# A two-layer transformer trunk on one core: the three inner layer norms and the first 512 columns of the stage behind each, in a written order of three engines

## The chip, the core and the metric

The kernel runs on one core of a Trainium2 chip. The metric is the device time of one execution in microseconds (us). A core has five engines, each with a queue of its own that runs in the order in which the instructions stand in it: TensorE (PE; its loads of stationary operands are listed apart as PEld), VectorE (DVE), ScalarE (ACT), GpSimd (POOL) and SyncE (SP, which here only issues DMAs). They wait for each other by semaphores.

## The reference

256 tokens of width 2048 pass through two layers. In each, a mixer is added to the scaled stream and normed, then a squared-ReLU MLP of hidden width 8192 is added and normed:

```python
for layer in range(DEPTH):                       # DEPTH = 2
    mix = fox_attention(...) if layer < 1 else nsa_attention(...)
    h = layer_norm(ALPHA * h + mix, ln1_g[layer], ln1_b[layer])
    h = layer_norm(ALPHA * h + sq_relu_mlp(h, mlp_w1[layer], mlp_w2[layer]), ln2_g[layer], ln2_b[layer])
    if layer == 0:
        kv = shared_kv(h, kv_w, ...)             # h @ kv_w: six parts of 512 columns, then compression
```

There are four layer norms. Behind the first and the third stands the MLP's first product (`h @ mlp_w1`, then the square of the ReLU), behind the second the product with `kv_w`, and behind the fourth only the output.

## The kernel before

**Arithmetic.** Each float32 operand is split into a high part (`hi`, the value rounded to the type fp32r) and a low part (`lo`, the rest). A product is hi x hi + hi x lo + lo x hi, accumulated in PSUM. Weights are streamed: `wload` loads half a chunk (128x1024, 512 KB) into one of 4 `raw` buffers, and `fill_split` makes `hi` by a cast on ScalarE (L117) and `lo` by a subtraction on VectorE (L118), into one of 5 `whl` buffers. This splitting goes on through the whole run, on the same two queues as everything else.

**Two forms of product.** In the form of `ws_many` the weights stand still and the 256 tokens stream by: for each of 16 parts of the inner dimension one matmul of 512 columns (L158: w hi against hi and lo of the tokens) and one of 256 (L160: w lo against hi). In the form of `xs_mm` 128 tokens stand still and 512 weight columns stream by: three matmuls of 512 columns for each part of the inner dimension and each half `t` of the tokens (L182). `out_proj` uses the second form for the projections that end in the stream `h`; `done` adds the accumulator to `h` and takes `bn_stats`.

**A junction** is the stretch from the last 512 columns (`n` = 3) of such a projection to the next stage's first products. The function `end` runs it. It keeps the last `LATE` = 4 half chunks of weights in a pool of their own, so that the products of the first 128 tokens (`t` = 0) end before those of the second (`t` = 1). After each half come `done`, `scalars` (mean and 1/sqrt(var + eps): small operations on VectorE, with one square root on ScalarE), then `columns`: two operations of VectorE on each 256 columns (L348 with the gain, L363 with the bias, each a row of 2048 numbers broadcast to 128 partitions by `gains`). `transposer` then turns each 512 columns with 4 matmuls against an identity (L376) into a PSUM tile `pt`, and splits them into the chunk `act` that the next stage reads. The next stage starts in the first form, whose every matmul needs both halves of the tokens. While TensorE has nothing to do there, it runs `tables` (in the first junction: two small products needed later, L597 and L600) or `warm` (in the second and third: `WARM` = 14 matmuls whose result nobody reads, L423). The fourth norm (`final`) divides its columns among VectorE, ScalarE and GpSimd.

**What sets the order.** The instructions are written in program order; a scheduler decides where each stands on its engine by priorities and modelled readiness.

Of the kernel before, what the change touches and what calls it, by code (L numbers as in the profile page):

```python
# [19 lines left out]
P = 128  # L20
S = 256
# [11 lines left out]
LATE = 4  # L33
WARM = 14
# [64 lines left out]
def _trunk(nc, tc, i, out, ctx):  # L99
# [78 lines left out]
    def xs_mm(acc, act, kt, t, w, first, last):  # L178
        s = slice(kt % 2 * 512, (kt % 2 + 1) * 512)
        xh, xl = (act[:, kt, k, t * P:(t + 1) * P] for k in range(2))  # L180
        for n, (l, r) in enumerate(((xh, 0), (xh, 1), (xl, 0))):
            mm(acc, l, w[:, r, s], start=first and n == 0, stop=last and n == 2)  # L182
# [8 lines left out]
    def merge(dst, acc, scale=1.0):  # L191

        t = sp.tile([P, S], F32, tag="mt", name="mt")
# [41 lines left out]
    def out_proj(src, acts, first, ln=None, two=False, between=()):  # L235
# [41 lines left out]
        def end(late, meanwhile=None):  # L277

            ln.gains(late)
            accs = [acc_tile(), acc_tile()]  # L280
            ahead = 8 - LATE
# [5 lines left out]
            ws = [wload(src[3, k // 2], k % 2, late, LATE) for k in range(ahead, 8)]  # L287
            for t in range(2):
                for kt in range(2 * ahead, KT):
                    xs_mm(accs[t], acts[kt // 4], kt % 4, t, ws[kt // 2 - ahead], False, kt == KT - 1)  # L290
# [5 lines left out]
                elif not ln.final:  # L296
                    ln.gained(1, 0)
            after = None
            if meanwhile:
                after = meanwhile()  # L300
            elif not ln.final:
                warm(WARM, ws[0][:, 0, :P], ws[0][:, 0, :512])
            with tc.issue_after(last):
                for t, c in ln.rest:
                    ln.columns(t, c)
                if after:
                    after()
        return end

    class Norm:  # L310


        def __init__(self, li, use, final=False):
            self.li, self.use, self.sc, self.had, self.final = li, use, {}, set(), final
            self.early = (2, 3, 0, 1) if final else (0,)
            self.rest = ((1, 3), (1, 0), (1, 1), (1, 2)) if final else (
                (1, 0), (0, 1), (1, 1), (0, 2), (1, 2), (0, 3), (1, 3))

        def scalars(self, t):
            mv = sp.tile([P, 6], F32, tag="mv", name="mv")  # L320
            nc.vector.bn_aggr(mv[:, 0:2], stats[:, t].rearrange("p c s -> p (c s)"))
            mean, var, v, y, a, rstd = (mv[:, k:k + 1] for k in range(6))
            nc.vector.tensor_scalar_add(v, var, EPS)
# [4 lines left out]
            end = nc.vector.tensor_mul(rstd, y, a)  # L328
            if self.final:
                end = nc.vector.scalar_tensor_tensor(a, mean, -1.0, rstd, op0=OP.mult, op1=OP.mult)  # L330
# [3 lines left out]
        def gains(self, pool):  # L334
            self.gb = []
            for name in ("lng", "lnb"):
                x = pool.tile([P, D], F32, name=name, bufs=1)
# [3 lines left out]
        def pieces(self, t, c):  # L341
            n = 512 if self.final else 256
            return [[x[:, a:a + n] for x in (h[:, t], *self.gb)] for a in range(c * 512, (c + 1) * 512, n)]

        def gained(self, t, c):
            self.had.add((t, c))
            for hs, g, _ in self.pieces(t, c):
                nc.vector.scalar_tensor_tensor(hs, hs, self.sc[t][0], g, op0=OP.subtract, op1=OP.mult)  # L348

        def columns(self, t, c):  # L350
            mean, rstd, nmr = self.sc[t]
            if self.final and (c == 3 or (t, c) == (0, 2)):
                hs, g, b = (x[:, c * 512:(c + 1) * 512] for x in (h[:, t], *self.gb))
# [6 lines left out]
            if (t, c) not in self.had:  # L360
                self.gained(t, c)
            for hs, _, b in self.pieces(t, c):
                nc.vector.scalar_tensor_tensor(hs, hs, rstd, b, op0=OP.mult, op1=OP.add)  # L363
            self.use(t, c)
            if self.final and (t, c) == self.rest[-1]:
                self.use(1, 3)
# [563 lines left out]
```

## Time and profile before

| | us |
|---|---|
| median of 3 runs (2247.07 to 2248.7) | 2247.33 |
| the profiled execution, its own time | 2248.41 |
| its span, first to last instruction | 2246.6 |
| busy in it: TensorE / VectorE / ScalarE | 2220.6 / 1408.0 / 1048.2 |

The page gives the busy time of each engine, then the costliest groups of instructions; a timeline lists the instructions of an engine in order, equal neighbours merged, and in square brackets how long the engine had stood idle and which instruction released it. PEclk is the granted clock of TensorE, 1.00 for 2.4 GHz and 0.50 for 1.2 GHz.

### The profile page before, as it was taken

To read this page: it belongs to the slowest core of one execution; us is meant where nothing else is said; L and a number is where in the kernel's file an instruction comes from. 1 tells how busy PE (TensorE), PEld (TensorE's weight loads), DVE (VectorE), ACT (ScalarE), POOL (GpSimd) and SP (SyncE) were. 2 spreads that over 40 slices of the span, in tenths; PEclk is the share of its full clock that TensorE was granted. 3 is DMA by queue.
4 is the path that set the end of the run, shared out by engine and by line. 5 is a ranking of instruction groups with operands and counts; after the bars stand their busy time and mean duration, and the time that the engine had idled before them with its cause. 6 is when DMAs were issued, how large, how long until landed. Compare 5 with 4: busy or idle time off the path is not lost.

```text
span 2246.6 us, 30144 instructions
## 1 busy us (share of the span) xinstructions
PE 2220.6 (99%) x11478; PEld 1893.7 (84%) x11478; DVE 1408.0 (63%) x2209; ACT 1048.2 (47%) x1564; POOL 18.6 (1%) x26
## 2 busy tenths in 40 slices
PE   9999999999999999999999999999999999999997
PEld 6888888888888888888788899888888888888885
DVE  5665556864665565565786688768655645655655
ACT  4444444443444454454355567544434434444542
POOL 0000000000000000000000000000000000000001
PEclk9999999999999999999999999999999999999999
DMA  7665567566666666666556744565666666666663
GB/s 253 196 197 188 178 188 249 198 190 192 192 191 192 193 188 195 190 188 194 179 165 221 246 134 137 168 217 170 192 192 190 191 193 194 189 193 191 189 196 112
DMA packets 116829, 427.54 MB, mean 190 GB/s; under 512 B 13179, under 2 KB 13339, under 8 KB 115406
## 3 DMA queue, kind: packets, MB, share of 16 engines
q1 hardware_dynamic: 114734, 419.00, 59.5%
q0 software_dynamic: 1952, 6.63, 1.0%
q8 instruction: 90, 1.47, 0.3%
q14 instruction: 53, 0.43, 0.1%
HBM read 423.45 MB, written 4.24 MB: 190 GB/s over the span
## 4 chain that ended last, share of the span: by engine, by line
PE 95%; DVE 2%; DMA 2%; ACT 0%; issue 0%; SPq 0%; ACTq 0%; DVEq 0%
PE acc L182 44%; PE acc L158 31%; PE acc L160 16%; DMA raw<-in_fq 1%; PE pt L839 1%; PE lg L775 0%; PE pt L817 0%; PE pt L376 0%; DMA raw<-in_fv 0%; DVE whl L118 0%; DMA bc<-c_dram 0%; DVE h L363 0%; PE acc L692 0%; PE pt L840 0%; PE pt L533 0%; PE lg L771 0%
## 5 line engine op out<-in xcount | busy, mean ns | idle before, releaser
L118 DVE TENSOR_TENSOR whl<-raw,whl 128x1024 fp32r<-128x1024 f32 (+1 forms) x769 | 938.4, 1223 | 613.6 <-ACT whl L117 605.0
L117 ACT CAST whl<-raw 128x1024 fp32r<-128x1024 f32 (+1 forms) x769 | 805.1, 1048 | 740.3 <-PE acc L182 491.6
L182 PE MATMUL acc<-whl,act 128*128 128x512 f32 x4416 | 1011.7, 390 | 2.2 <-DVE whl L118 1.2
L182 PEld LDWEIGHTS acc<-whl,act 128*128 128x128 f32 x4416 | 827.1, 188 | 177.6 <-DVE whl L118 2.8
L158 PE MATMUL acc<-act,whl 128*128 128x512 f32 x3072 | 757.3, 394 | 0.0
L158 PEld LDWEIGHTS acc<-act,whl 128*128 128x128 f32 x3072 | 563.5, 189 | 107.3 <-issue 0.2
L160 PEld LDWEIGHTS acc<-act,whl 128*128 128x128 f32 x3072 | 398.2, 191 | 16.9 <-DVE whl L118 0.3
L160 PE MATMUL acc<-act,whl 128*128 128x256 f32 x3072 | 408.7, 284 | 0.0
L194 ACT ACTIVATE mt<-acc 128x256 f32<-128x256 f32 x192 | 73.4, 382 | 299.7 <-PE acc L158 297.5
L196 DVE TENSOR_TENSOR mu<-acc,mt 128x256 f32<-128x256 f32 x128 | 54.4, 425 | 113.4 <-ACT mt L194 113.4
L394 DVE SCALAR_TENSOR_TENSOR mu<-mu 128x256 f32<-128x256 f32 x128 | 54.4, 425 | 4.3
L118 DVE TENSOR_TENSOR act<-mu,act 128x256 fp32r<-128x256 f32 x128 | 53.7, 420 | 0.0
L117 ACT CAST act<-mu 128x256 fp32r<-128x256 f32 x128 | 52.1, 407 | 3.1 <-DVE mu L394 1.6
L117 ACT CAST act<-pt 128x256 fp32r<-128x256 f32 x80 | 29.4, 372 | 41.9 <-PE pt L376 31.3
L250 DVE TENSOR_TENSOR h<-h,acc 128x512 f32<-128x512 f32 x48 | 30.9, 681 | 14.2 <-PE acc L182 14.2
L118 DVE TENSOR_TENSOR act<-pt,act 128x256 fp32r<-128x256 f32 x80 | 33.1, 419 | 9.9 <-ACT act L117 9.6
L404 ACT ACTIVATE E<-E,sm 128x128 f32<-128x128 f32 (+1 forms) x64 | 28.9, 453 | 7.8 <-DVE sm L407 7.4
L363 DVE SCALAR_TENSOR_TENSOR h<-h,mv,lnb 128x256 f32<-128x256 f32 (+1 forms) x53 | 26.5, 541 | 0.1
L404 ACT ACTIVATE E<-L,sm 128x128 f32<-128x128 f32 (+1 forms) x32 | 14.3, 449 | 24.8 <-DVE sm L407 24.8
L376 PE MATMUL pt<-cst,h 128*128 128x128 f32 x96 | 19.1, 293 | 6.0 <-DVE h L363 6.0
L348 DVE SCALAR_TENSOR_TENSOR h<-h,mv,lng 128x256 f32<-128x256 f32 (+1 forms) x53 | 25.0, 502 | 0.0
L248 DVE SCALAR_TENSOR_TENSOR h<-h,acc 128x512 f32<-128x512 f32 x32 | 20.6, 681 | 4.2 <-PE acc L182 4.2
(173 smaller groups left out, 664.0 us busy)
## 6 DMA issues: line engine op xcount, KB each, us to landing
raw<-in_w SPq DMA_DIRECT2D x512, 512.0 KB, 3.6
raw<-in_fq SPq DMA_DIRECT2D x32, 512.0 KB, 3.7
raw<-in_fk SPq DMA_DIRECT2D x32, 512.0 KB, 3.6
raw<-in_fo SPq DMA_DIRECT2D x32, 512.0 KB, 4.0
raw<-in_kvT SPq DMA_DIRECT2D x32, 512.0 KB, 4.4
raw<-in_nq SPq DMA_DIRECT2D x32, 512.0 KB, 3.7
raw<-in_no SPq DMA_DIRECT2D x32, 512.0 KB, 4.1
raw<-in_fv SPq DMA_DIRECT2D x31, 512.0 KB, 3.7
```

The costliest lines, as they stand in the source:

```text
L117: nc.scalar.copy(hi, src)
L118: nc.vector.tensor_sub(lo, src, hi.bitcast(F32))
L158: mm(acc, w[:, 0, s], a, start=kt == 0, stop=kt == KT - 1)
L160: mm(acc[:, :S], w[:, 1, s], a[:, 0, :], start=False, stop=False)
L182: mm(acc, l, w[:, r, s], start=first and n == 0, stop=last and n == 2)
L194: nc.scalar.activation(t, acc[:, S:], AF.Copy, scale=scale)
L196: nc.vector.tensor_add(dst, acc[:, :S], t)
L250: nc.vector.tensor_add(hcols(t, n), hcols(t, n), acc)
L348: nc.vector.scalar_tensor_tensor(hs, hs, self.sc[t][0], g, op0=OP.subtract, op1=OP.mult)
L363: nc.vector.scalar_tensor_tensor(hs, hs, rstd, b, op0=OP.mult, op1=OP.add)
L394: nc.vector.scalar_tensor_tensor(u, u, 0.0, u, op0=OP.max, op1=OP.mult)
L404: nc.scalar.activation(E, L, AF.Exp, bias=m, scale=-1.0, accum_out=sums)
```

## The change

The fourth norm keeps its code; only `LATE`, the number of weight half chunks held back, becomes 7 for it too, and its gain and bias tiles come from another pool. The three inner norms get a new function `joined` and a class `Turned`:

- The next stage's first 512 columns (of `mlp_w1`, laid out a second time as `w1r`, or of the part of `kv_w` called `kvN`) are computed in the second form, by halves of the tokens: 96 matmuls into `nxt[0]` and `nxt[1]`, in the order (0,0) (0,1) (0,2) (1,0) (0,3) (1,1) (1,2) (1,3) of pairs (half `t`, 512 columns `c` of the inner dimension), 12 matmuls each. The held weights are 7 half chunks (5 in the first junction, with the `tables` behind the products).
- Each pair has six steps: `norm` on ScalarE (one operation on 128x512, without gain and bias), `turn` on TensorE (4 transposes), `gained` on VectorE and on ScalarE (gain and bias as one number per partition, from `lnT`, on the 128x128 transposes in PSUM; 2 of 4 on VectorE for `t` = 0, 3 of 4 for `t` = 1), `hi` on ScalarE, `lo` on VectorE. `PIECES` gives each step a place. The unit of a place is one matmul of TensorE, and 0 is the first of the next stage.
- Everything in the junction is sorted by place and handed to TensorE, VectorE and ScalarE in that order, past the scheduler; the splits of three of the new weight half chunks stand among it.
- `h` stays without gain and bias for a while; `residual` applies them behind the second 128-column product of the next stage: 8 operations of VectorE on 128x1024, which wait for `lng` and `lnb`.
- In the MLP the two accumulators are 128 tokens by 512 hidden columns. They pass ReLU (ScalarE), square (VectorE), 8 transposes (TensorE) and a split.
- The warm matmuls go. The product with `kvN[0]`, which stood behind the others of its stage, now comes first in it. The buffers of `mt` and `mu` go from 2 to 1.

```diff
-LATE = 4
-WARM = 14
+LATE = 7
+BETWEEN = 11
+PIECES = {
+    (0, 0): (-24, -20, -18, -18, -13, -9),
+    (0, 1): (-23.5, -15, -14, -9, -5, -1),
+    (0, 2): (-12, -6, -5, -2, 3, 10),
+    (0, 3): (12, 15, 31, 23, 34, 36),
+    (1, 0): (20, 23, 27, 27, 32, 34),
+    (1, 1): (36, 41, 47, 45, 52, 56),
...
+        def joined(late, first, held, between=None):
+            accs, products = begun(late, held)
+            ws = {(c, k): wload(first[c], k) for c, k in ((0, 0), (0, 1), (1, 0), (1, 1), (2, 0))}
+            nxt = [acc_tile(), acc_tile()]
+            ln.open()
+            at = []
+            add = lambda place, go: at.append((place, len(at), go))
+            room = BETWEEN if between else 0
+            for n, go in enumerate(products):
+                add(n - len(products) - room, go)
...
+            order = ((0, 0), (0, 1), (0, 2), (1, 0), (0, 3), (1, 1), (1, 2), (1, 3))
+            n = 0
+            for t, c in order:
+                for kt in range(4):
+                    for k in range(3):
+                        add(n, lambda t=t, c=c, kt=kt, k=k: xs_mm(
+                            nxt[t], ln.cs[c], kt, t, ws[c, kt // 2], c == kt == 0, c == kt == 3, (k,)))
+                        n += 1
+            for c, k, hi, lo in ((2, 1, 6, 19), (3, 0, 15, 40), (3, 1, 40, 45)):
+                raw, w = raw_tile(), late.tile([P, 2, HALF], F32R, tag="whl", name="whl", bufs=held)
...
+                add(hi, lambda raw=raw, w=w: nc.scalar.copy(w[:, 0], raw))
+                add(lo, lambda raw=raw, w=w: nc.vector.tensor_sub(w[:, 1], raw, w[:, 0].bitcast(F32)))
+            for t in range(2):
+                place = -len(products) - room if t == 0 else 0.5 - room
+                for d, go in ((0, lambda t=t: done(3, t, accs[t])), (0, lambda t=t: ln.scalars1(t)),
+                              (10.5, lambda t=t: ln.scalars2(t))):
+                    add(place + d, go)
...
+            with tc.manual_schedule(engines={mybir.EngineType.PE, mybir.EngineType.DVE, mybir.EngineType.Activation}):
+                for place, _, go in sorted(at, key=lambda x: x[:2]):
+                    go()
...
+            def gained(ks, vector):
+                tp, x = got
+                for k in ks:
+                    g, b = (lnT[:, self.li, n, 4 * c + k:4 * c + k + 1] for n in range(2))
+                    src = tp[:, k * P:(k + 1) * P]
+                    if vector:
+                        nc.vector.tensor_scalar(x[:, k], src, g, b, op0=OP.mult, op1=OP.add)
+                    else:
+                        nc.scalar.activation(x[:, k], src, AF.Identity, bias=b, scale=g)
...
+        def residual(self):
+            self.gains(ap, tag="act")
+            for t in range(2):
+                for a in range(0, D, HALF):
+                    hs, g, b = (x[:, a:a + HALF] for x in (h[:, t], *self.gb))
+                    nc.vector.tensor_mul(hs, hs, g)
+                    nc.vector.tensor_add(hs, hs, b)
```

TensorE at the second junction (from the first MLP into the product with `kv_w`), before. `L182` are the last products of the projection, `L376` the transposes, `L423` the warm matmuls, and `L158` and `L160` the next stage.

```order
L182 MATMUL acc<-whl,act 128x512 x377
L376 MATMUL pt<-cst,h 128x128 x4
L182 MATMUL acc<-whl,act 128x512 x7
L423 MATMUL idle<-whl 128x512 x14
L376 MATMUL pt<-cst,h 128x128 x8
L158 MATMUL acc<-act,whl 128x512 x8
L160 MATMUL acc<-act,whl 128x256 x2
```

The same place now. `L195` is the second form in the new file, `L450` the transposes of a pair, and `L170` the stage's further products.

```order
L195 MATMUL acc<-whl,act 128x512 x365
L450 MATMUL pt<-cst,h 128x128 x4
L195 MATMUL acc<-whl,act 128x512 x5
L450 MATMUL pt<-cst,h 128x128 x4
L195 MATMUL acc<-whl,act 128x512 x9
L450 MATMUL pt<-cst,h 128x128 x4
L195 MATMUL acc<-whl,act 128x512 x21
L450 MATMUL pt<-cst,h 128x128 x4
L195 MATMUL acc<-whl,act 128x512 x8
L450 MATMUL pt<-cst,h 128x128 x4
L195 MATMUL acc<-whl,act 128x512 x18
L450 MATMUL pt<-cst,h 128x128 x4
```

The transposes of the first three pairs now stand among the 42 products of the second half, and those of the others among the next stage's own matmuls; no warm matmul is left between.

ScalarE at the same junction, before: `L324` is the square root, `L117` the splits.

```order
L324 ACTIVATE mv<-mv 128x1
L117 CAST act<-pt 128x2x128 x2
L324 ACTIVATE mv<-mv 128x1
L117 CAST act<-pt 128x2x128 x8
L117 CAST whl<-raw 128x1024
L117 CAST act<-pt 128x2x128
L117 CAST whl<-raw 128x1024
```

The same place now, from the middle of it on: `L354` is the split of a weight half chunk inside the junction, `L394` the square root (here that of the second half), `L445` a pair's `norm`, `L460` its `gained`, `L465` its `hi`, and `L129` the split of a half chunk of the products that follow.

```order
L460 ACTIVATE lx<-pt,lnT 128x128 x2
L465 CAST act<-lx 128x4x128
L354 CAST whl<-raw 128x1024
L394 ACTIVATE mv<-mv 128x1
L445 ACTIVATE h<-h,mv 128x512
L354 CAST whl<-raw 128x1024
L445 ACTIVATE h<-h,mv 128x512
L460 ACTIVATE lx<-pt,lnT 128x128 x3
L465 CAST act<-lx 128x4x128 x2
L445 ACTIVATE h<-h,mv 128x512
L354 CAST whl<-raw 128x1024
L129 CAST whl<-raw 128x1024
```

ScalarE now carries norm, gain and split of the pairs, with the casts of weights between them.

VectorE behind the second junction, now: `L209` adds the parts of a 128-column product, `L472` and `L473` are `residual`.

```order
L130 TENSOR_TENSOR whl<-raw,whl 128x1024
L209 TENSOR_TENSOR rawT<-acc,mt 128x256
L130 TENSOR_TENSOR whl<-raw,whl 128x1024 x2
L209 TENSOR_TENSOR rawT<-acc,mt 128x256
L472 TENSOR_TENSOR h<-h,lng 128x1024 x3
L473 TENSOR_TENSOR h<-h,lnb 128x1024 x3
L472 TENSOR_TENSOR h<-h,lng 128x1024
L209 TENSOR_TENSOR rawT<-acc,mt 128x256
L473 TENSOR_TENSOR h<-h,lnb 128x1024
L130 TENSOR_TENSOR whl<-raw,whl 128x1024 x2
```

Before, no such block stood there. It now stands between two groups of weight splits (`L130`).

## Rows read from the trace of the kernel before

**Rows 1.** the page: one engine, and one group (busy, mean, idle before)
```profile
PE 2220.6 (99%) x11478; PEld 1893.7 (84%) x11478; DVE 1408.0 (63%) x2209; ACT 1048.2 (47%) x1564; POOL 18.6 (1%) x26
...
L376 PE MATMUL pt<-cst,h 128*128 128x128 f32 x96 | 19.1, 293 | 6.0 <-DVE h L363 6.0
```

**Rows 2.** timeline of TensorE, first junction: start, us, instruction, count, [idle before]
```profile
397.87 0.82 PE L597 MATMUL rps<-oh 99*16 99x384 f32 x2
...
403.68 1.12 PE L376 MATMUL pt<-cst,h 128*128 128x128 f32 x4 [2.64 <-DVE h L363]
...
405.72 2.73 PE L158 MATMUL acc<-act,whl 128*128 128x512 f32 x8
```

**Rows 3.** timeline of TensorE, second junction
```profile
1114.27 3.37 PE L423 MATMUL idle<-whl 128*128 128x512 f32 x14
...
1120.50 3.65 PE L158 MATMUL acc<-act,whl 128*128 128x512 f32 x8
```

**Rows 4.** timeline of TensorE, third junction
```profile
1516.10 3.38 PE L423 MATMUL idle<-whl 128*128 128x512 f32 x14
...
1522.80 3.43 PE L158 MATMUL acc<-act,whl 128*128 128x512 f32 x8
```

**Rows 5.** two of three alike stretches: us, busy by engine, PEclk, DMA share, GB/s
```profile
403.66:407.07 3.41, 3.22 (x11) 2.43 (x12) 3.07 (x8) 1.02 (x3) 0.00 (x0) 0.50 0.98 339
...
1523.23:1526.64 3.41, 3.41 (x11) 2.73 (x10) 2.97 (x8) 0.72 (x3) 0.00 (x0) 0.50 0.00 0
```

**Rows 6.** chain that ended last, after the first junction: start, us, work, count
```profile
409.03 0.22 PE pt L376 x2
...
424.71 2.75 PE acc L158 x12
427.46 1.91 PE acc L160 x16
```

**Rows 7.** timeline of VectorE, norm of the first 128 tokens, second junction
```profile
1108.12 0.69 DVE L250 TENSOR_TENSOR h<-h,acc 128x512 f32<-128x512 f32 x1 [2.77 <-PE acc L182]
...
1110.79 0.21 DVE L326 SCALAR_TENSOR_TENSOR mv<-mv 128x1 f32<-128x1 f32 x1
...
1111.22 0.16 DVE L328 TENSOR_TENSOR mv<-mv 128x1 f32<-128x1 f32 x1
```

**Rows 8.** timeline of ScalarE, first junction
```profile
401.08 0.56 ACT L608 COPY cb<-cbps 128x480 f32<-128x480 f32 x1 [1.89 <-PE cbps L600]
401.54 0.21 ACT L324 ACTIVATE mv<-mv 128x1 f32<-128x1 f32 x1
```

**Rows 9.** groups by line and shape, VectorE: busy us, mean ns, idle before
```profile
L118 DVE TENSOR_TENSOR whl<-raw,whl 128x1024 fp32r<-128x1024 f32 x767 | 937.0, 1224 | 611.5 <-ACT whl L117 602.9
...
L802 DVE TENSOR_SCALAR E<-E,sm 128x128 f32<-128x128 f32 x32 | 9.0, 281 | 0.0
...
L118 DVE TENSOR_TENSOR vhl<-acc,vhl 128x512 fp32r<-128x512 f32 x2 | 1.4, 692 | 0.7 <-ACT vhl L117 0.7
```

**Rows 10.** groups by line and shape, ScalarE
```profile
L117 ACT CAST whl<-raw 128x1024 fp32r<-128x1024 f32 x767 | 803.8, 1049 | 738.1 <-PE acc L182 491.6 <-PE acc L160 164.7 <-issue 32.2
...
L354 ACT ACTIVATE h<-h,mv 128x512 f32<-128x512 f32 x3 | 2.3, 810 | 4.7 <-DVE mv L330 4.7
```

**Rows 11.** timeline of VectorE and GpSimd at the end of the span
```profile
2233.91 1.25 POOL L355 TENSOR_TENSOR h<-h,lng 128x512 f32<-128x512 f32 x1
...
2234.13 1.05 DVE L326 SCALAR_TENSOR_TENSOR mv<-mv 128x1 f32<-128x1 f32 x1
...
2235.41 1.12 DVE L328 TENSOR_TENSOR mv<-mv 128x1 f32<-128x1 f32 x1
```

**Rows 12.** DMA issues by line: count, KB each, median us from issue to landing
```profile
raw<-in_w SPq DMA_DIRECT2D x512, 512.0 KB, 3.6
...
lnb<-in_lnb SPq DMA_DIRECT2D x4, 1024.0 KB, 8.1
```

More of the change, by code (lines that the diff above doesn't have):

```diff
@@ L176, in ws_stream, with xs_mm @@
             j += n
[L178 removed]
+    def xs_mm(acc, act, kt, t, w, first, last, which=range(3)):
         s = slice(kt % 2 * 512, (kt % 2 + 1) * 512)
         xh, xl = (act[:, kt, k, t * P:(t + 1) * P] for k in range(2))
[L181 removed]
+        for n in which:
+            l, r = ((xh, 0), (xh, 1), (xl, 0))[n]
             mm(acc, l, w[:, r, s], start=first and n == 0, stop=last and n == 2)
@@ L275, in out_proj, with begun @@
                 ended(n, accs)
-        def end(late, meanwhile=None):
-            ln.gains(late)
+        def begun(late, held):
             accs = [acc_tile(), acc_tile()]
-            ahead = 8 - LATE
+            ahead = 8 - held
             for k in range(ahead):
@@ L308, in out_proj, with __init__ @@
+        end.joined = joined
         return end
     class Norm:
[L313 to L317, printed above, removed]
+        early = (2, 3, 0, 1)
+        rest = ((1, 3), (1, 0), (1, 1), (1, 2))
+        def __init__(self, li, use):
+            self.li, self.use, self.sc, self.had = li, use, {}, set()
@@ L359, in columns @@
                 return
[L360 to L363, printed above, removed]
+            nc.vector.scalar_tensor_tensor(hs, hs, mean, g, op0=OP.subtract, op1=OP.mult)
+            nc.vector.scalar_tensor_tensor(hs, hs, rstd, b, op0=OP.mult, op1=OP.add)
             self.use(t, c)
-            if self.final and (t, c) == self.rest[-1]:
+            if (t, c) == self.rest[-1]:
@@ L584, in _trunk @@
         xs = []
-        end = out_proj(i["fo"], oc, True, Norm(0, transposer(xs)), True, [lambda k=k: run(k) for k in range(n, n + 3)])
+        ln = Turned(0, xs)
+        end = out_proj(i["fo"], oc, True, ln, True, [lambda k=k: run(k) for k in range(n, n + 3)])
     with tc.tile_pool(name="late", bufs=2) as late:
@@ L609, in tables @@
             return keep_them
-        end(late, tables)
+        accs = end.joined(late, i["w1r"][0], LATE - 2, tables)
     acts, xs = xs, []
-    mlp(0, acts, Norm(1, transposer(xs)))
+    ln, before = Turned(1, xs), ln
+    accs = mlp(0, acts, accs, before, ln, i["kvN"][0])
     with tc.tile_pool(name="np", bufs=2) as np_:
@@ L859, in _trunk @@
         acts = []
-        end = out_proj(i["no"], oc, True, Norm(2, transposer(acts)), True, [lambda k=k: run(k) for k in range(n, n + 4)])
+        ln = Turned(2, acts)
+        end = out_proj(i["no"], oc, True, ln, True, [lambda k=k: run(k) for k in range(n, n + 4)])
     with tc.tile_pool(name="late", bufs=2) as late:
-        end(late)
-    mlp(1, acts, Norm(3, to_output, True))
+        accs = end.joined(late, i["w1r"][1], LATE)
+    mlp(1, acts, accs, ln, Norm(3, to_output))
 def laid_out(a):
```

177 lines of the change are left out of this document (116 added, 61 removed), and 2 rows, old and new, of the table PIECES.

## Prediction

> **What bounds the kernel now.** I read the page first. TensorE is busy 2220.6 of 2246.6 us, VectorE 63% and ScalarE 47% [rows 1]. Nothing is to be won by relieving VectorE or ScalarE on the average: only what lets TensorE wait, or gives it work to no purpose, counts. The page shows where it waits: of its groups with transposes, L376 stood 6.0 us idle, released by VectorE's L363, the second half of the norm [rows 1]. Then I read TensorE's timeline at the three inner norms. In each the reader is to see a gap between the last product of the old stage and the first L158 of the new one: 397.87 to 405.72 in the first junction [rows 2], 1114.27 to 1120.50 in the second [rows 3], 1516.10 to 1522.80 in the third [rows 4]. In the first, `tables` fill it until 401.04 (403.68 less 2.64 of idle time); in the others 14 warm matmuls of 3.4 us do, which serve nothing. Last I read the granted clock in the stretches behind: three times it stands at 0.50, 1.2 GHz, for 3.41 us, right after these gaps of idling [rows 5], and the eight L158 that begin at 1120.50 take 3.65 us [rows 3], where twelve take 2.75 at full clock [rows 6].
>
> **What is removed.** The gaps are 7.85 less 3.17 for the tables, that is 4.68; 6.23; and 6.70: 17.6 us [rows 2 to 4]. In them lie 24 useful transposes at 0.11 us [rows 6], 2.6 us, which the new kernel needs too. 15.0 us remain. The low clock costs half its length where products run in it: 405.72 to 407.07 in the first junction, 0.7 us; nearly the whole 3.4 us in the others, 1.7 each: 4.1 us [rows 2 to 5]. Together 19.1 us, if TensorE finds work all through and keeps its clock.
>
> **Does it find work?** A matmul of 512 columns takes 0.229 us in the stream (2.75 / 12) and one of 256 columns 0.119 (1.91 / 16) [rows 6]. I walk through the second junction; the third is like it.
>
> First half of the tokens: VectorE's chain from `done` to 1/sqrt ran from 1108.12 to 1111.38, 3.26 us, with two operations of the old norm in between [rows 7]. One more small operation (the mean times 1/sqrt, 0.16 by its like) makes 3.45, the new `norm` 0.81 (L354 is the same operation on the same shape [rows 10]): 4.3 us. The transposes of pair (0,0) stand 22 matmuls behind the half's last product, 5.0 us. That leaves 0.7.
>
> Second half, counted from its last product: the same 3.45 us, and on VectorE the `lo` of (0,2) in front of the small operations, 0.69 [rows 9]: 4.1. On ScalarE the square root comes before the chain's last five small operations, at about 2.4; behind it stand the norm of (0,3), 0.81, and a weight cast, 1.05 [rows 10], then the norm of (1,0): done at about 5.1. Its transposes stand at place 23, 23 x 0.229 plus 4 transposes, 5.7. VectorE has a weight split (1.22) in front of the gains and is through with it at 5.4; three gains at 0.28 each after the transposes end (6.2), `hi` at most 0.81, `lo` 0.69 [rows 9, 10]: 8.6. Place 36 with 8 transposes comes at 9.1, and wants `hi`; `lo` is wanted two matmuls later. This is the tightest chain by length, and it holds by half a microsecond.
>
> Pair (1,1) is tighter: two casts for the further products stand in ScalarE's queue before its `hi`, and wait for `whl` buffers that TensorE frees at places 42 and 48. Casts, one norm (0.81), one gain and `hi` follow each other from place 42 on and end near place 58 to 60; `lo`, behind two splits on VectorE, near place 62, where it is wanted.
>
> The gain on a 128x128 piece of PSUM is not in the trace. From below nothing; from above one operation on 512 columns. I take 0.28 on VectorE (L802, the same operation from SBUF [rows 9]). From the second half's last product to its last piece VectorE then has 7 weight splits of 1.22, 6 `lo` of 0.69, 14 gains of 0.28 and the chain of 3.45: 20.0 us, while TensorE has 96 x 0.229 plus 20 transposes, 24.2. So it keeps up. The Trainium skill, "VectorE: DVE Perf Modes", section "Why PSUM operands drop a tier", says that an fp32 operand in PSUM gets no faster mode, while L802 reads SBUF. Taken at its worst, with every gain at twice the row, VectorE would have 23.9 us for the same 24.2, and the waits below would be about 1 us longer in each junction, 3 us in all; I keep to the row.
>
> For such misses by some tenths I put 0.5 us of new waits into each junction, +1.5 us; the ends are 0 and about 2 each.
>
> **The first junction** has a slower ScalarE: the two copies of `tables` stand in its queue, and the second waited 1.89 us for TensorE [rows 8]. Now it stands in front of steps of (0,2) and of the second half's square root. The tables give the chain 11 places more, and it comes out as tight as the others.
>
> **Weights.** The first half's 42 products use a held half chunk each 6 x 0.229 = 1.4 us, faster than TensorE uses them elsewhere (12 products, 2.75 us). The seven held buffers are filled meanwhile, since four raw half chunks lie ready and each load lands 3.6 us after its issue [rows 12]. I cost this at nothing; without that stock, each missing chunk would cost about 1.4 us.
>
> **Smaller terms.** The new form: 96 x 0.229 = 22.0 us where 64 x (0.229 + 0.119) = 22.3 stood, -0.3 in each MLP, -0.6. The eight transposes of the hidden columns: 16 x 0.11 = +1.8. `residual` is 8 operations like a 128x1024 split, 9.8 us of VectorE at 1.22 [rows 9], hidden behind weights already split: four half chunks of 8 x (0.229 + 0.119) = 2.8 us, 11.1 us. If that cover is gone, each half chunk costs up to 2.8.
>
> At the end of the span, two small operations on VectorE take 1.05 and 1.12 us while GpSimd works on the first half's columns [rows 11]; their likes took 0.21 and 0.16 [rows 7]. With 42 instead of 24 products between the halves GpSimd starts 4.1 us earlier relative to the second half and is through before these two: -1.8. The bounds are 0 and -1.8.
>
> **Sum.** -19.1 - 0.6 + 1.8 - 1.8 + 1.5 = -18.2 us. The profiled execution took 2248.41, so 2230.2; the median of the runs, 2247.33, lies 1.1 below it. I forecast 2229.1.
>
> **Rivals.**
> - *A cast in the way.* ScalarE runs its queue in order: the square root at 401.54 came right behind a copy that had waited 1.89 us [rows 8]. If a cast of a further half chunk waits for its load or its buffer, the pair's steps behind it are late, and TensorE with them. The load reuses the raw buffer that VectorE frees about place 19; 3.6 us of landing put it at place 35 to 40, the cast is wanted near 47. In the first junction the DMA engines are 98% busy behind the tables [rows 5], with the write of `b_dram` that the tables feed. At 2 us of stall and 1.7 of low clock per junction, 3 x 3.7 less the 1.5 already counted: +9.6, 2238.7. The Trainium skill, "TensorE: Matmul & The Clock Gate", section "Architectural detail", calls the queues of ScalarE and VectorE strict FIFO; by that rule this is how a miss would spread, and rows 8 agree.
> - *residual empties the stock of weights.* The block with its neighbours is 10.6 us and the next split 1.2; four ready half chunks and the eight wide matmuls that need no `lo` cover 11.1 + 1.8. With three ready, TensorE stalls 1.7 us and loses 1.7 to the clock: 3 x 3.4 = +10.2, 2239.3. For it speaks the loaded VectorE just before; against it that it has 4 us of slack in 24.
> - *Slower.* VectorE's queue stands still at `residual` until `lng` and `lnb` have landed. They are issued behind ten weight half chunks, and `lnb` took 8.1 us to land [rows 12]. I put its issue some 8 us before the first operation of `residual`, so the wait is near zero. To lose all 18.2 us and 4.5 more, each junction must lose 7.6: 5.9 of standing still and 1.7 of clock, that is `lnb` landing 12 us after `residual` begins (1.1 of margin, 4 operations with the gain first, 5.9). With 2 us more than that in each, 2258.
> - *Nothing won.* The norm's chain is as long as before, and a miss at (1,0) of 5 to 6 us with its low clock would give the gaps back: about 2246. The walk has it the other way round by half a microsecond; a miss that size needs every duration on the chain half as long again.
>
> **How the numbers follow.** My forecast 0.76, with its own range 2226 to 2234 (2227.6 without new waits, and 1.5 less if the old junctions also lost some tenths outside the gaps; 2233.6 with 2 us of waits in each); a cast in the way 0.10; the empty stock 0.07; nothing won 0.03; slower 0.04. A measurement of this kernel can tell 0.2%, 4.5 us, from no change. So faster 0.93, same 0.03, slower 0.04. The range must leave out no more than 2 in 10: 2226 to 2239 takes in the forecast and about half of the first two rivals.
>
> **What would show it.** The three stretches of clock 0.50 gone; no L423 of warm matmuls inside; the idle time before the transposes of the pairs under 1 us per junction; the first products of the new stage less than 1 us after the old one's last; TensorE's span between these ends filled at 0.229 us a matmul. At the end, the small operations at 0.2 us. I am wrong if the low clock is still there, if ScalarE's casts L129 wait in a junction with `hi` behind them, or if TensorE idles for a VectorE split some 10 to 15 us behind `residual`'s start.

## The result and the profile after

| | before | after |
|---|---|---|
| median, us | 2247.61 (2247.07 to 2248.7, 4 runs) | 2231.49 (2230.72 to 2233.57, 4 runs) |
| profiled execution: its span, us | 2246.6 | 2229.5 |
| mean granted clock of TensorE | 0.995 | 0.998 |

The change made the kernel 16.1 us faster, ratio 0.9929, 95% interval 0.9912 to 0.9946. The forecast was 2229.1 in a range of 2226 to 2239: right in sign and mechanism, and 2.4 us too low, in part by a step that had been given no price (below).

The page of the changed kernel: the engines, then the gains of the pairs on VectorE and on ScalarE.

```profile
PE 2209.8 (99%) x11402; PEld 1883.6 (84%) x11402; DVE 1408.0 (63%) x2163; ACT 1072.6 (48%) x1592; POOL 18.7 (1%) x26
...
L458 DVE TENSOR_SCALAR lx<-pt,lnT 128x128 f32<-128x128 f32 x60 | 21.0, 404 | 19.4 <-PE pt L450 19.2
...
L460 ACT ACTIVATE lx<-pt,lnT 128x128 f32<-128x128 f32 x36 | 15.0, 449 | 13.4 <-DVE lx L458 13.4
```

TensorE's timeline at the first and second junctions, which answers to [rows 2, 3]. `L195` are the 512-column products, `L450` the transposes of a pair; the first two rows are of the first junction.

```profile
401.90 3.92 PE L195 MATMUL acc<-whl,act 128*128 128x512 f32 x16
406.19 0.66 PE L450 MATMUL pt<-cst,h 128*128 128x128 f32 x4 [0.37 <-ACT h L445]
...
1110.48 5.03 PE L195 MATMUL acc<-whl,act 128*128 128x512 f32 x21
1115.35 0.60 PE L450 MATMUL pt<-cst,h 128*128 128x128 f32 x4
1115.71 2.10 PE L195 MATMUL acc<-whl,act 128*128 128x512 f32 x8
1117.64 0.60 PE L450 MATMUL pt<-cst,h 128*128 128x128 f32 x4
1118.00 4.53 PE L195 MATMUL acc<-whl,act 128*128 128x512 f32 x18
```

In the second junction each row begins before the one above has drained, and no bracket of idle time stands anywhere. The third reads the same. The first has one wait, 0.37 us, for the norm of pair (0,3). The granted clock, in windows over the three junctions (us, busy of PE, PEld, DVE, ACT and POOL, PEclk, DMA share, GB/s), against [rows 5]:

```profile
380.00:440.00 60.00, 59.63 (x305) 49.24 (x305) 41.39 (x73) 36.20 (x57) 1.53 (x2) 1.00 0.63 212
1095.00:1145.00 50.00, 50.00 (x248) 41.30 (x247) 33.87 (x63) 29.10 (x48) 1.85 (x3) 1.00 0.51 166
1495.00:1545.00 50.00, 50.00 (x255) 41.73 (x254) 35.08 (x66) 31.19 (x49) 0.00 (x0) 1.00 0.49 168
```

The end of the span, against [rows 11]: GpSimd is through with the first half's columns at 2217.43, and the second half's small operations on VectorE take 0.22 and 0.16 us.

```profile
2216.16 1.27 POOL L416 TENSOR_TENSOR h<-h,lnb 128x512 f32<-128x512 f32 x1
...
2218.96 0.22 DVE L396 SCALAR_TENSOR_TENSOR mv<-mv 128x1 f32<-128x1 f32 x1
...
2219.40 0.16 DVE L398 TENSOR_TENSOR mv<-mv 128x1 f32<-128x1 f32 x1
```

TensorE's waits over the whole span (line, what it waited for: us in total, times, longest) show what is left:

```profile
PE acc L195 <- DVE whl L130: 2.0, 4, 0.8
...
PE pt L640 <- DVE E L631: 1.1, 1, 1.1
...
PE pt L450 <- ACT h L445: 0.4, 1, 0.4
```

**Where the time went.** For each shape of matmul I took its usual distance from start to next start, the median over the trace (0.227 us for 512 columns), and added these up. What remains between the first matmul's start and the last's is waiting and low clock, sorted by stretches; the junctions are 390 to 430, 1090 to 1140 and 1490 to 1550 us. The forecast's terms, sorted in the same way, stand beside it: 28 warm matmuls are 6.4 us of its 19.1.

| us | before | after | difference | forecast |
|---|---|---|---|---|
| matmuls at their usual distance | 2192.3 | 2186.8 | -5.5 | -6.4 - 0.6 + 1.8 = -5.2 |
| waiting and low clock, three junctions | 14.8 | 2.7 | -12.1 | -12.7 + 1.5 = -11.2 |
| waiting and low clock elsewhere | 22.8 | 25.2 | +2.4 | 0 |
| last matmul's start to the end | 15.3 | 13.4 | -1.9 | -1.8 |

The junctions gave 0.9 us more than forecast and the matmuls 0.3; 2.4 us were given back in places that the forecast had no term for. Most of it, +1.9, is the difference over the whole stage behind the second junction (1140 to 1490 us: 5.3 before, 7.2 after). The largest waits there stand in the compression behind the moved `kvN[0]` product; TensorE's timeline there:

```profile
1244.35 3.94 PE L195 MATMUL acc<-whl,act 128*128 128x512 f32 x16 [0.53 <-DVE whl L130]
...
1263.79 1.19 PE L825 MATMUL acc<-whl,winhl 128*120 128x512 f32 x4 [0.66 <-DVE whl L130]
...
1279.36 1.96 PE L866 MATMUL pt<-cw,xw 128*96 128x128 f32 x16 [0.69 <-DVE xw L853]
```

Another 0.7 lies in the first 40 us, where executions differ: the 31st matmul starts at 14.06 us in the kernel before, at 14.69 in the changed one, and at 14.08 in a variant with the same start (e_best, below). The rest, -0.2, is in small waits.

### The profile page after: what moved, and what is told of

Read it like the earlier page. It is cut to its first block, busy times and chain, and to the rows that moved or that the text cites. A ratio compares the mean times of both kernels' runs of the same rounds, so it can differ in the third digit from the quotient of the medians.

```text
span 2229.5 us, 30071 instructions
## 1 busy us (share of the span) xinstructions
PE 2209.8 (99%) x11402; PEld 1883.6 (84%) x11402; DVE 1408.0 (63%) x2163; ACT 1072.6 (48%) x1592; POOL 18.7 (1%) x26
## 4 chain that ended last, share of the span: by engine, by line
PE 95%; DMA 2%; DVE 2%; ACT 1%; issue 0%; SPq 0%; ACTq 0%; DVEq 0%
PE acc L195 46%; PE acc L170 29%; PE acc L172 15%; DVE whl L130 1%; PE pt L971 1%; PE pt L949 1%; PE lg L907 0%; PE pt L450 0%; ACT whl L129 0%; DMA raw<-in_fv 0%; DMA bc<-c_dram 0%; DMA raw<-in_kvN 0%; DMA raw<-in_xT 0%; PE pt L972 0%; PE pt L654 0%
## 5 line engine op out<-in xcount | busy, mean ns | idle before, releaser
L130 DVE TENSOR_TENSOR whl<-raw,whl 128x1024 fp32r<-128x1024 f32 (+1 forms) x760 | 927.7, 1223 | 587.4 <-ACT whl L129 578.3
L129 ACT CAST whl<-raw 128x1024 fp32r<-128x1024 f32 (+1 forms) x760 | 796.2, 1048 | 729.8 <-PE acc L195 476.3
L195 PE MATMUL acc<-whl,act 128*128 128x512 f32 x4608 | 1062.8, 391 | 2.4 <-DVE whl L130 2.0
L195 PEld LDWEIGHTS acc<-whl,act 128*128 128x128 f32 x4608 | 861.9, 188 | 185.4 <-DVE whl L130 3.8
L170 PE MATMUL acc<-act,whl 128*128 128x512 f32 x2944 | 719.8, 393 | 0.0
L170 PEld LDWEIGHTS acc<-act,whl 128*128 128x128 f32 x2944 | 538.9, 188 | 103.3 <-issue 0.2
L172 PEld LDWEIGHTS acc<-act,whl 128*128 128x128 f32 x2944 | 378.3, 191 | 14.9 <-DVE whl L130 0.4
L172 PE MATMUL acc<-act,whl 128*128 128x256 f32 x2944 | 385.8, 283 | 0.0
L209 DVE TENSOR_TENSOR mu<-acc,mt 128x256 f32<-128x256 f32 x120 | 50.9, 424 | 106.6 <-ACT mt L207 106.2
L129 ACT CAST act<-mu 128x256 fp32r<-128x256 f32 x120 | 48.9, 407 | 4.8 <-DVE mu L488 3.4
L130 DVE TENSOR_TENSOR act<-mu,act 128x256 fp32r<-128x256 f32 x120 | 50.1, 417 | 0.0
L458 DVE TENSOR_SCALAR lx<-pt,lnT 128x128 f32<-128x128 f32 x60 | 21.0, 404 | 19.4 <-PE pt L450 19.2
L524 ACT ACTIVATE E<-L,sm 128x128 f32<-128x128 f32 (+1 forms) x32 | 14.3, 449 | 25.2 <-DVE sm L527 25.2
L527 DVE CUSTOM_DVE_ANT_0 E<-lg,nbm 128x128 f32<-128x128 f32 (+1 forms) x64 | 22.4, 351 | 0.2
L460 ACT ACTIVATE lx<-pt,lnT 128x128 f32<-128x128 f32 x36 | 15.0, 449 | 13.4 <-DVE lx L458 13.4
L265 DVE BATCH_NORM_STATS2 stats<-h 128x6 f32<-128x512 f32 x32 | 21.2, 685 | 0.3
L445 ACT ACTIVATE h<-h,mv 128x512 f32<-128x512 f32 x24 | 19.1, 810 | 3.2 <-DVE mv L399 3.2
```

Of the source, the lines that this page charges most:

```text
L129: nc.scalar.copy(hi, src)
L130: nc.vector.tensor_sub(lo, src, hi.bitcast(F32))
L170: mm(acc, w[:, 0, s], a, start=kt == 0, stop=kt == KT - 1)
L172: mm(acc[:, :S], w[:, 1, s], a[:, 0, :], start=False, stop=False)
L209: nc.vector.tensor_add(dst, acc[:, :S], t)
L524: nc.scalar.activation(E, L, AF.Exp, bias=m, scale=-1.0, accum_out=sums)
```

## The experiments

My theory was the forecast's: the junctions' gaps are filled because the new form lets TensorE work on one half while the other is normed, and the written order makes that hold by some tenths. The rivals: the halves alone do it, whatever the order; the held chunks do it; the gain is only the warm matmuls' time.

### What fills the gaps

**e_nowarm**: the kernel before without its warm matmuls.

```diff
-            elif not ln.final:
-                warm(WARM, ws[0][:, 0, :P], ws[0][:, 0, :512])
```

> The kernel before without its 28 warm matmuls. Theory (they fill a wait that is there anyway): the gaps stay 6.2 and 6.7 us long, idle time before the transposes rises by about 3.2 us in the second and third junction, and the time stays within 2 us, plus or minus what the clock does: if the stretch of half clock starts earlier but is not longer, part of it falls into the gap and the time can even drop by 1 to 2 us; if it lasts twice as long, +3.4 us. Rival (the warm matmuls take time of their own): the time drops by up to 6.4 us.

2249.44 (2247.26 to 2252.58, 10 runs), ratio 1.0009 (0.9999 to 1.0019). The warm matmuls' time turned into waiting: their 6.75 us [rows 3, 4] went, and the wait before the transposes grew from 6.0 [rows 1] to 11.9 us. The low clock stayed, and was longer in two junctions, one of them the first, which the edit does not touch. The page, then two of three windows at low clock:

```profile
L374 PE MATMUL pt<-cst,h 128*128 128x128 f32 x96 | 20.1, 315 | 11.9 <-DVE h L361 11.9
```

```profile
401.20:408.03 6.83, 6.03 (x19) 4.66 (x20) 6.04 (x16) 1.39 (x4) 0.00 (x0) 0.50 0.93 296
...
1517.40:1524.23 6.83, 4.25 (x13) 3.00 (x14) 6.57 (x22) 1.59 (x5) 0.00 (x0) 0.50 0.00 0
```

So dropping `warm` is not the gain; the gap is.

**e_sched**: the changed kernel with the same calls in the same program order, placed by the scheduler.

```diff
-            with tc.manual_schedule(engines={PE, DVE, Activation}):
-                for place, _, go in sorted(at, key=lambda x: x[:2]):
-                    go()
+            for place, _, go in sorted(at, key=lambda x: x[:2]):
+                go()
```

> The changed kernel without the written order: the same instructions in the same program order, but the scheduler decides where each stands on TensorE, VectorE and ScalarE. Theory (computing by halves gives the cover, and the written order is needed to use it): weight casts and splits slip in front of the pairs' steps, TensorE stops for some us in each junction, and the time rises by 6 to 15 us. Rival (the halves alone give all of it): within 2 us of the changed kernel, with as little idle time at the transposes.

2231.67 (2230.12 to 2232.59, 4 runs), ratio 0.9926 (0.9911 to 0.9941): the changed kernel's time. ScalarE's order is another one: at the second junction it does four norms in one block, where the written order puts gains and splits between. ScalarE's timeline:

```profile
1106.21 2.93 ACT L444 ACTIVATE h<-h,mv 128x512 f32<-128x512 f32 x4 [1.56 <-DVE mv L398]
```

TensorE waits 0.2 us there at most, and the clock stays at 1.00. **The theory fell here**: the written order is not what wins. That leaves the halves and the held chunks.

**e_held4**: e_sched with four held half chunks at the three inner junctions, so 24 products behind the first half instead of 42 (30 in the first junction). The rest of the first half's scalars moves up to the half's start, as they no longer fit 10.5 places later.

```diff
-                              (10.5, lambda t=t: ln.scalars2(t))):
+                              (10.5 * t, lambda t=t: ln.scalars2(t))):
...
-            return end.joined(late, first, LATE) if first is not None else end(late)
+            return end.joined(late, first, 4) if first is not None else end(late)
...
-        accs = end.joined(late, i["w1r"][0], LATE - 2, tables)
+        accs = end.joined(late, i["w1r"][0], 4, tables)
...
-        accs = end.joined(late, i["w1r"][1], LATE)
+        accs = end.joined(late, i["w1r"][1], 4)
```

> The run in which the scheduler sets the order, with 4 held half chunks instead of 7 (5 in the first junction) at the three inner norms: 24 matmuls, 5.5 us, of the second half stand behind the first half's last product instead of 42, 9.6 us. Theory (the halves only hide the norm as far as held products cover it: from the first half's last product to the first split piece the chain needs about 7 us, with the longer gains that the trace shows): TensorE stops for about 1.5 to 2 us in the second and third junction and less in the first, where the tables stand too; +3 to +9 us with the clock. Rival (the halves of the next stage are the cover, and the held chunks add nothing): within 1 us of the run with the scheduler's order.

2244.72 (2241.44 to 2246.21, 10 runs), ratio 0.9986 (0.9977 to 0.9995): 13 us of the 16 are lost. TensorE's timeline at the second junction, and the windows at low clock:

```profile
1103.79 8.41 PE L195 MATMUL acc<-whl,act 128*128 128x512 f32 x36
1114.85 1.82 PE L449 MATMUL pt<-cst,h 128*128 128x128 f32 x8 [2.65 <-ACT h L444]
1117.75 1.11 PE L449 MATMUL pt<-cst,h 128*128 128x128 f32 x4 [1.08 <-ACT lx L459]
```

```profile
1115.50:1122.33 6.83, 5.70 (x19) 4.44 (x19) 4.33 (x13) 6.83 (x15) 0.00 (x0) 0.50 0.18 73
1521.70:1525.11 3.41, 3.41 (x11) 2.79 (x10) 2.80 (x10) 2.73 (x6) 0.00 (x0) 0.50 0.12 44
```

The products of the second half run out before the first half's columns are there: 18 fewer of them are 4.1 us less cover. I had expected less, for I counted the stops and not the low clock behind them: by start-to-start distances the stops are 1.4, 4.2 and 3.0 us, and half of 10.2 us at low clock is 5.1, of which a part falls into the stops. So the halves of the tokens win little without the longer reserve of products: of the 2.5 us that this run still lies under the kernel before, 1.9 are the tail's, which kept its seven chunks. The reserve without the halves, seven held chunks in the kernel before, was not tried. That it alone would not fill the gap is argued: in the kernel before, the gap stands behind the last product of the second half [rows 2 to 4], and the next stage's first form needs both halves.

### How much slack

**e_chain6** and **e_chain3**: six, and three, operations without use (`bn_stats`, 0.69 us each) on VectorE ahead of the second half's chain.

```diff
+            junk = sp.tile([P, 6], F32, tag="junk", name="junk", bufs=1)
+            for k in range(6):                                    # 3 in e_chain3
+                add(0.5 - room, lambda: nc.vector.bn_stats(junk, hcols(1, 3)))
```

> The changed kernel with six more bn_stats on VectorE behind the second half's own in each of the three junctions (results unused): 6 x 0.69 = 4.1 us more on the chain of the second half. Theory (the chain has a slack of some tenths to 1.2 us against TensorE's work): a stop of TensorE of about 3 us before pair (0,3) or (1,0) in each junction, +9 us in all, and +14 if the granted clock falls behind each stop. Rival (several us of slack are left, since VectorE is busy for 20 of 24 us only): under +3 us in all.

> The changed kernel with three more bn_stats on the second half's chain, 2.06 us. From the run with six, where 4.1 us gave stops of 2.85 to 2.97 us, the slack is about 1.2 us. Theory (slack, then one for one): stops of 0.8 to 0.9 us in each junction, +2.6 us, and no fall of the clock. Rival (any stop of that place lets the clock fall): +2.6 and about 1.7 for each junction, +7.7.

e_chain6: 2244.83 (2242.13 to 2247.03, 10 runs), ratio 0.9984 (0.9975 to 0.9994). With 4.1 us more on VectorE, TensorE stopped for 2.97, 2.85 and 2.84 us more than usual, so some 1.2 us were slack. In the second and third junctions it stopped before the transposes of pair (1,0), which is the second half's chain. In the first it was another one: there the added operations stand ahead of the `lo` of pair (0,0) on VectorE, and TensorE stopped before the third matmul of the next stage, the first that wants a `lo`.

```profile
403.90 5.08 PE L195 MATMUL acc<-whl,act 128*128 128x512 f32 x14 [2.80 <-DVE act L468]
```

After two of the three stops the clock fell, after the third it didn't; windows of e_chain6 behind the three stops:

```profile
404.39:407.80 3.41, 3.41 (x10) 2.64 (x9) 2.84 (x9) 3.02 (x6) 0.00 (x0) 0.50 1.02 353
1124.60:1128.01 3.41, 3.41 (x10) 2.67 (x9) 2.79 (x8) 2.50 (x5) 0.00 (x0) 0.50 0.51 154
1525.00:1528.41 3.41, 3.41 (x18) 2.68 (x16) 2.35 (x7) 2.16 (x6) 0.00 (x0) 1.00 0.50 154
```

Ten matmuls in 3.41 us at 0.50, eighteen at 1.00 (four of these are transposes). e_chain3: in the second and third junctions 2.06 us more gave stops of 0.7 us (the bracket of the second says 0.51), hence 1.4 of slack, and the clock stayed at 1.00 in all three junctions.

```profile
1119.62 0.66 PE L453 MATMUL pt<-cst,h 128*128 128x128 f32 x4 [0.51 <-ACT h L448]
```

So the chain of the second half has about 1.3 us of slack in the second and third junctions; beyond it TensorE stopped one for one, and a stop of 2.85 us could cost low clock on top.

e_chain3's one run took 2237.08, 5.6 us more than the changed kernel, where 2.6 were expected. By start-to-start distances the junctions' stops are 2.3 of it. Most of the rest lies outside the chain: TensorE waited 1.07 us in the first layer, with 3.41 us at 0.50 behind it, and 1.15 us behind the second junction, for a weight split behind `residual`, which itself had waited 2.52 us for the load of `lng`. In the changed kernel the same wait of VectorE was 0.81 us. TensorE in e_chain3, with the window at low clock; then `residual`'s start in e_chain3 and in the changed kernel:

```profile
42.75 0.40 PE L585 MATMUL pt<-lf,cst 128*128 128x16 f32 x2 [1.07 <-DVE lf L581]
...
1163.77 2.36 PE L172 MATMUL acc<-act,whl 128*128 128x256 f32 x16 [1.15 <-DVE whl L130]
```

```profile
44.49:47.90 3.41, 3.41 (x15) 3.21 (x15) 0.31 (x1) 0.77 (x1) 0.69 (x1) 0.50 0.55 173
```

```profile
1153.07 3.50 DVE L475 TENSOR_TENSOR h<-h,lng 128x1024 f32<-128x1024 f32 x3 [2.52 <-DMA lng<-in_lng]
```

```profile
1149.23 3.50 DVE L472 TENSOR_TENSOR h<-h,lng 128x1024 f32<-128x1024 f32 x3 [0.81 <-DMA lng<-in_lng]
```

**e_nores** leaves `residual` and its loads of `lng` and `lnb` out (the stream is then without gain and bias of the three inner norms); **e_res2** applies them twice (the stream gets both twice).

```diff
 e_nores
-            self.gains(ap, tag="act")
-            for t in range(2):
+            for t in ():
 e_res2
-                    nc.vector.tensor_mul(hs, hs, g)
-                    nc.vector.tensor_add(hs, hs, b)
+                    for _ in range(2):
+                        nc.vector.tensor_mul(hs, hs, g)
+                        nc.vector.tensor_add(hs, hs, b)
```

> The changed kernel without residual: the stream keeps the normed values without gain and bias in the three inner norms, and lng and lnb are not loaded there. Theory (the block of 9.8 us on VectorE is covered by weights already split): within 1 us of the changed kernel. Rival (it empties the stock of split weights): 3 us or more faster, with fewer waits for L130 behind the junctions.

> The changed kernel with the operations of residual doubled: 19.6 us instead of 9.8 on VectorE behind each junction (gain and bias applied twice, so the stream has other values). Theory (the cover ends about 1 us behind the single block): TensorE stops for a split L130 for some 8 us in each junction, and its clock falls behind that; +25 to +32 us. Rival (the cover is larger, because the casts on ScalarE and TensorE's other work go on): under +15 us.

e_nores: 2231.51 (2229.78 to 2233.07, 4 runs), ratio 0.9926 (0.9911 to 0.9941), no faster: `residual` is covered, and its two loads with it. e_res2: 2258.24 in its one run. TensorE stood before a product that wanted a weight split from behind the doubled block; its waits, the second of them in the timeline, and the clock behind:

```profile
PE acc L172 <- DVE whl L130: 20.1, 3, 6.9
```

```profile
1165.60 5.63 PE L170 MATMUL acc<-act,whl 128*128 128x512 f32 x24
1177.58 3.78 PE L172 MATMUL acc<-act,whl 128*128 128x256 f32 x16 [6.35 <-DVE whl L130]
```

```profile
1175.70:1182.50 6.80, 4.92 (x20) 4.63 (x21) 6.80 (x7) 1.05 (x1) 0.00 (x0) 0.50 0.49 157
```

By start-to-start distances the stops are 7.0, 6.5 and 7.0 us. The margin of `residual` is not the difference to 9.8: eight operations back to back take 9.1 us (the block of the first junction runs from 439.54 to 458.79 here, from 439.99 to 450.15 in the changed kernel), and 24 products of 512 columns stand ahead of the stop here, against 16 in the changed kernel, 1.8 us more cover. 9.1 less 1.8 less 7.0 leaves 0.3. The changed kernel's own trace says the same: the first split behind the block ends at 451.62, and the product that wants it starts at 451.91, 0.3 us later.

```profile
450.40 1.22 DVE L130 TENSOR_TENSOR whl<-raw,whl 128x1024 fp32r<-128x1024 f32 x1
...
451.91 1.12 PE L172 MATMUL acc<-act,whl 128*128 128x256 f32 x8
```

So the block is covered with at most 0.3 us to spare in the first junction, and as little in the third (1557.67 and 1557.97).

### The tail

**e_tail4**: the changed kernel, the fourth norm with four held half chunks again.

```diff
-            accs, products = begun(late, LATE)
+            accs, products = begun(late, 4)
```

> The changed kernel, with 4 instead of 7 held half chunks at the fourth norm alone. Theory (the tail is shorter because GpSimd is through before the second half's small operations): the two small VectorE operations take about 1.05 and 1.12 us again instead of 0.2, and the stretch from TensorE's last matmul to the end of the span grows from 13.3 to about 15.2 us; in all +1.9 us. Rival (the tail is shorter by chance, or for the order of VectorE's queue): the stretch stays at 13.3 us.

2234.61 (2234.39 to 2234.93, 4 runs), ratio 0.994 (0.9925 to 0.9955). From the last matmul's start to the end it is 15.3 us, where the changed kernel has 13.4: the 1.9 us expected. The rest of the 3.1 between the medians is not in the tail; in the two traces most of it lies in waits before 80 us. Timeline of VectorE and GpSimd:

```profile
2220.66 1.16 DVE L396 SCALAR_TENSOR_TENSOR mv<-mv 128x1 f32<-128x1 f32 x1
2221.84 0.15 DVE L397 TENSOR_SCALAR mv<-mv 128x1 f32<-128x1 f32 x1
2222.03 1.11 DVE L398 TENSOR_TENSOR mv<-mv 128x1 f32<-128x1 f32 x1
...
2220.54 1.25 POOL L415 TENSOR_TENSOR h<-h,lng 128x512 f32<-128x512 f32 x1
2221.87 1.26 POOL L416 TENSOR_TENSOR h<-h,lnb 128x512 f32<-128x512 f32 x1
```

The two long operations, of one element for each partition, end at 2221.82 and 2223.14, when GpSimd's end (2221.79 and 2223.13); L397, with one input, between them takes its 0.15. The Trainium skill, "SBUF — State Buffer", section "Who interferes with whom", says that a VectorE instruction with two inputs in SBUF contends with a GpSimd instruction that reads SBUF; this trace agrees. The price here was the rest of GpSimd's instruction, both times.

### A better version

**e_spread**: the second compression behind head 0's `nq` product, its later steps behind the next runs of products, so that no VectorE operation stands just ahead of a matmul that wants it. **e_best**: that, and the norm of (0,3) at place 4 instead of 12, ahead of a weight cast on ScalarE. **after_again** and **e_best_again** repeat the changed kernel and e_best side by side.

```diff
 e_spread
-        steps = {0: lambda: cmp.update({0: compress(0)}), 1: lambda: cmp[0][0](), 3: lambda: cmp[1][0]()}
+        steps = {0: lambda: cmp.update({0: compress(0)}), 1: lambda: cmp[0][0](), 2: lambda: cmp[0][1]()}
...
-            if kc == 2:
-                cmp[0][1]()
-                cmp[1] = compress(1)
-            else:
+            if kc in steps:
...
-        at(1, cmp[1][1])
+        at(1, lambda: cmp.update({1: compress(1)}))
+        at(2, lambda: cmp[1][0]())
+        at(3, lambda: cmp[1][1]())
 e_best, besides
-    (0, 3): (12, 15, 31, 23, 34, 36),
+    (0, 3): (4, 15, 31, 23, 34, 36),
```

> The changed kernel with the second compression (32 matmuls for 8 half chunks of weights) moved behind the first head's product with nq, and its two later steps one and two steps behind that, so that it no longer stands 48 matmuls behind the first. Theory (putting the kvN[0] product first has left the two compressions too close together, and TensorE takes their weights faster than they are split: about 2 us of waits near 1240 to 1280): the waits there fall below 0.6 us, -1.5 to -2 us. Rival (the waits belong to the compression itself, as before the change): the same 2 us, further behind.

> As the run with the compression moved, and the norm of pair (0,3) at place 4 instead of 12, ahead of a weight cast on ScalarE. Theory: the 0.4 us that TensorE waits for this norm in the first junction go too; in all 2 to 2.5 us under the changed kernel. Rival: the cast that is now behind makes pair (1,0) late, and the 0.4 us come back there.

> The changed kernel again, beside the version with the compression moved: 2231.5 us as before.

> The version with the compression moved and the norm of (0,3) earlier, again: 2.0 us under the changed kernel on the same chip, as the two traces show it (losses of 26.5 against 28.6 us).

e_spread: 2230.82 (2230.37 to 2236.64, 4 runs), ratio 0.9932 (0.9915 to 0.9949). The waits of `L866` and `L825` were gone, that near 1243 stayed, and a new one came. By start-to-start distances the stretch from 1235 to 1330 us lost as much as in the changed kernel, 4.4 against 4.5 us, so the fall of 1.5 to 2 us that I expected did not come. TensorE's timeline:

```profile
1243.66 5.28 PE L195 MATMUL acc<-whl,act 128*128 128x512 f32 x22 [0.52 <-DVE whl L130]
...
1294.43 0.36 PE L965 MATMUL pt<-pc,vc 96*128 96x256 f32 x1 [0.74 <-DVE pc L952]
```

e_best: 2229.46 (2228.4 to 2231.46, 4 runs), ratio 0.9918 (0.9904 to 0.9933). Side by side, five runs each: after_again 2230.85 (2229.86 to 2231.58), ratio 0.9927 (0.9915 to 0.994); e_best_again 2229.17 (2228.82 to 2231.76), ratio 0.9921 (0.9907 to 0.9935). The wait of (0,3), 0.4 us, is gone in both traces. The 1.7 us between the medians lie inside the spread of the runs, and the moved compression explains none of them (its stretch lost 4.5 us in e_best and 5.2 in e_best_again, against 4.4 in after_again), so a gain beyond that wait is not shown.

## Why the prediction was right, and where it was off

**The gaps, the low clock and the warm matmuls** (-19.1): right. The three stretches at 0.50 are gone, with the warm matmuls, and the new stage's first products follow the old one's last without a gap. The new waits came to 0.4 us, less than the 1.5 allowed.

**The chains.** The walk put the second half's slack at half a microsecond; e_chain3 and e_chain6 show 1.3 in the second and third junctions. On ScalarE the norm of (1,0) ended 4.5 us after the half's first VectorE operation in the second junction (1116.50 and 1112.01), where 5.1 were counted: the square root came 0.3 us earlier, and the operations behind it overlapped by 0.1 us each. The walk named (1,0) and (1,1) as the tightest; the only miss is (0,3) in the first junction. Its norm stands behind a weight cast in ScalarE's queue, which `tables` had made late; ScalarE's timeline of the changed kernel:

```profile
401.73 0.56 ACT L731 COPY cb<-cbps 128x480 f32<-128x480 f32 x1 [0.84 <-PE cbps L723]
...
404.38 1.05 ACT L354 CAST whl<-raw 128x1024 fp32r<-128x1024 f32 x1
405.32 0.81 ACT L445 ACTIVATE h<-h,mv 128x512 f32<-128x512 f32 x1
```

This is the rival of a cast in the way, at a tenth of its price; e_best moved the norm ahead of the cast and the wait went.

**The gains** were mis-sized: 0.404 us on VectorE (21.0 / 60 is 0.35 where they overlap) and 0.449 on ScalarE, instead of 0.28. The row from SBUF was the wrong like. The Trainium skill, "VectorE: DVE Perf Modes", section "Why PSUM operands drop a tier", says that an fp32 operand in PSUM is held to the lowest of the speed modes; this trace agrees in direction, at 1.4 times the row from SBUF and not the twofold that I took as its worst. It cost nothing, since VectorE still kept up.

**residual** was costed at nothing, and e_nores shows no cost. But the margin was at most 0.3 us in the first and third junctions, not the 1.1 of the forecast, so that term held in part by luck. The cover was mis-sized: from the block's start to the product that wants the split it is 11.9 us (439.99 to 451.91), where 12.9 were counted. The rival of the emptied stock came that near. Of the rival *Slower* the wait exists, for `lng` and not for `lnb`: VectorE stood 0.81 us in the second junction, without a stop of TensorE, and 2.52 us in e_chain3, with one of 1.15. No run shows a wait for `lnb`.

**The tail** (-1.8): -1.9 in the trace, undone by e_tail4, for the reason given.

**The step that failed** is one without a number: the moved `kvN[0]` product was told among the change's parts and never priced. It shifts the compression against the weight splits, and the stage cost 1.9 us more. e_spread removed two of the three waits and lost as much in others, so the cost is not that of these waits' places alone. That the move caused it was not tried. The sum closes: -18.2 as forecast, -0.3 in the matmuls, -0.9 in the junctions' waits, -0.1 in the tail and +2.4 elsewhere are -17.1, the difference of the spans. The median moved by 1.0 less than the spans, since the profiled execution of before lay above its median and that of after did not; so 2.4 us of miss are 1.1 of forecast, 1.0 of this, and 0.3 from a median of before that came out higher.

**What I believed beyond the forecast**, that the written order was needed, fell with e_sched. With 42 products in reserve, the scheduler's order did as well.

## What to carry to other kernels

Here a norm between two products was hidden by splitting both the end of the old product and the beginning of the new one by tokens, with enough products of the second half held back to cover the first half's chain (42 did, 24 did not): count both in microseconds and compare. Dropping filler matmuls alone won nothing. A run that doubles a piece of work measures its margin only if the order around it stays: compare what stands ahead of the stop. Price every instruction that a change moves, also the one that seems a mere reordering: here time came back beside the one move that had no price.

## What the runs showed of the hardware that I had not expected

The clock's answer did not follow the length of a stop: after stops of 2.97 and 2.85 us in e_chain6 it stood at 0.50 for 3.41 us, after one of 2.84 it stayed at 1.00; after 0.7 us in e_chain3's junctions it stayed. In the first layer it was the other way: behind the stop of 1.07 us in e_chain3 (above) it fell, and behind one of 1.36 us at the same place in e_best_again it stayed:

```profile
43.30 0.40 PE L582 MATMUL pt<-lf,cst 128*128 128x16 f32 x2 [1.36 <-DVE lf L578]
```

```profile
44.40:47.80 3.40, 3.40 (x25) 2.89 (x23) 0.62 (x3) 1.05 (x1) 0.69 (x1) 1.00 0.65 194
```

In the kernel before it fell in all three junctions [rows 5].

A VectorE operation on one element for each partition took 1.16 us instead of 0.22 when it met GpSimd, and ended within 0.03 us of GpSimd's operation.
